# Down-weight sums called at later places, and eight tiles for the last residual loads, in an fp32 hybrid decoder layer

## The chip, the core and the metric

One core of one Trainium2 chip runs the whole program. Its engines are TensorE (PE in the trace; it loads weights as PEld), VectorE (DVE), ScalarE (ACT), GpSimd (POOL) and SyncE (SP). Each engine runs its own instructions in order and waits on semaphores for the others. The metric is the device time of one execution in microseconds, the median of the runs.

## The reference, cut to what matters

One decoder layer over 2048 tokens of width 1024, all in float32. The `mixer` part is a gated spatial unit (8 heads) beside a chunkwise matrix-memory LSTM (4 heads); then comes a channel mixer with a causal convolution over 2 x 2816 columns, then a gated embedding and a last norm.

```python
h = rms_norm(x, g_mix[i])
u, v, qk, vm, o, ig, fg = jnp.split(h @ w_in[i], cuts, axis=-1)
...
x = x + jnp.concatenate([gm, ml], axis=-1) @ w_out[i]
h = rms_norm(x, g_ffn[i])
up = causal_dwconv(h @ w_up[i], ffn_conv_w[i], ffn_conv_b[i])
a, bv = jnp.split(up, 2, axis=-1)
x = x + (jax.nn.silu(a) * bv) @ w_down[i]
gate = jax.nn.sigmoid(rms_norm(x, g_ple[i]) @ w_ple_gate[i])
x = x + gate * (p[i] @ w_ple[i])
```

## The kernel before

**Products.** Every float32 matrix is split into a high and a low part (ScalarE copies the high part, DVE subtracts it from the original to get the low one), and every product is three matmuls: high by high, high by low, low by high.

**Mixer.** A loop `b` = 0 to 3 takes 512 tokens at a time. In each block come four token groups (`w_v` columns, evacuated to `gv`, `vm1`, `osig` and the gates `gt`), the gate chain, then the query/key and `u` tiles with four heads (state update `cn`, denominators `dd`, head output `hc`), and the out-projection: eight steps `d`, each with one `w_out` slice, a load of the residual `xr` from `xT` (L681), the DVE add of residual and product (L682), and a store of the result to `x1s` (L683). Block 0 takes its input unnormed and puts the norm on while it evacuates, so it has more DVE work than the others. In the course of a block the squares and the norm of the next block's input are made (`xs` loads, `sq`, `sh`, `sl`). The eight residual tiles of a block rotate through two buffers with the tag `xr`.

**FFN.** 1024 tokens at a time: `up_half(0)`, `down_half(0)`, `up_half(1)`, `down_half(1)`. An up half runs over 22 columns `j` of 128; each `j` is computed by seven products of halves in place of eight (a Strassen form), in the order 1, 2, 6, 5, 7, 3, 4. The operands of its products are the split up weights `sw` (from `wr`, with adds at L803, L804 and L808) and the split inputs `tt` (from `hx`, which holds stored sums `td` of the normed input). After products DVE works on the results `ua` and `ub` (L855, L861 and others), makes the convolution (`fc`) and, for each pair of columns, the sums `two` of the activations, which go to memory as `ad`. For j = 8, 10, 12, 14 the step `last_in` prepares the FFN input of the last mixer block (`xl`, `hl`, further `two` tiles).

**Sums of the down weights.** The down halves use the same seven-product form and need sums of `w_down`: for each of 11 pairs `k`, `sums_load(k)` loads two 512 KB slices into two tiles `ds0`, `ds1` (one buffer each, L256) and `sums_make(k)` makes four sums of 128x512 on DVE (L262 to L265) and stores them, 256 KB each, to `sd_3`, `sd_5`, `sd_6`, `sd_7` (L267). `down_half` reads them later. They are called three in a block: 3b and 3b+1 at the token groups 1 and 3, and 3b+2 among the heads.

**What sets the order.** The Tile scheduler lists each engine's instructions. It takes an instruction as soon as its inputs and its buffers are free by its own reckoning, so a call's place in the code is not its place on an engine. Loads go through SP's queue (`DMA = nc.sync`), nearly all stores through POOL's (`ST = nc.gpsimd`); a store that waits holds what stands behind it on POOL, and so does a load on SP. A tile that is reused waits for all readers of its last contents, stores to memory included. Tiles of the FFN lie in the storage that the mixer's tiles had.

Of the kernel before, what the change touches and what calls it, by code (L numbers as in the profile page):

```python
# [9 lines left out]
F32 = mybir.dt.float32  # L10
# [5 lines left out]
P = 128  # L16
# [25 lines left out]
def trunk_kernel(ctx: ExitStack, tc: tile.TileContext, xT, pT, w_u, w_qk, w_v0, w_v1,  # L42
# [208 lines left out]

    def sums_load(k):
        if k < NJ // 2:
            dsum[k] = [big.tile([P, 2, TB], F32, tag=f"ds{i}", name=f"ds{i}") for i in range(2)]
            for i, t in enumerate(dsum[k]):
                DMA.dma_start(t, w_down[2 * k + i].rearrange("p (i t) -> p i t", t=TB))  # L256

    def sums_make(k):

        if k < NJ // 2:  # L260
            p, q = dsum.pop(k)
            V.tensor_tensor(q[:, 1, :], p[:, 1, :], q[:, 1, :], ALU.add)  # L262
            V.tensor_tensor(p[:, 1, :], p[:, 0, :], p[:, 1, :], ALU.subtract)
            V.tensor_tensor(p[:, 0, :], q[:, 1, :], p[:, 0, :], ALU.subtract)
            V.tensor_tensor(q[:, 0, :], q[:, 0, :], p[:, 0, :], ALU.subtract)  # L265
            for n, t in ((5, q[:, 1, :]), (7, p[:, 1, :]), (6, p[:, 0, :]), (3, q[:, 0, :])):
                ST.dma_start(sds[n][:, k, :], t)  # L267

    with mx:
# [3 lines left out]
        def tt(nm, dt=F32):  # L273
            return tp.tile([P, TB], dt, tag="t", name=nm, bufs=NT)
# [69 lines left out]
        for b in range(NB):  # L344
# [117 lines left out]

            sums_load(3 * b)
            ps = tok_group(1, {0: [chain1], 1: [chain2], 2: [chain3]} | ({3: [pend[0].st2]} if b else {}))
# [3 lines left out]

            sums_make(3 * b)
            ps = tok_group(2, ({2: [nx.st2]} if b + 1 < NB else {}) | ({1: [pend[0].st3]} if b else {}))  # L470
# [12 lines left out]
            for t in range(CPB):  # L483
                V.tensor_scalar(gv[:, t, :], gv[:, t, :], mu[:, t, 0:1], lrs[:, t:t + 1], ALU.subtract, ALU.mult)
            sums_load(3 * b + 1)
            ps = tok_group(3)
            for t in range(CPB):
                evac(osig[:, t, 128:512], ps[t][:, 0:384], t)
            sums_make(3 * b + 1)
            if b:  # L490
# [131 lines left out]
            k1, o0 = qk_tile(5, lambda f: head_b(*a, f))  # L622
            sums_load(3 * b + 2)
            g1 = u_tile(1)
# [4 lines left out]
            k2, o1 = qk_tile(6, lambda f: head_b(*a, f))  # L629
            sums_make(3 * b + 2)  # L630
            g2 = u_tile(2)
# [40 lines left out]
            nf = SumSq(tp, "t", NT, V)  # L672
            for d in range(KD):
                if d < 2:
                    ps = first[d][0]
                else:
                    w = wsplit(w_out[d], 1024)
                    ps = acc()
                    wide(ps, w, cat, (4, 5, 6, 0, 1, 2, 3, 7))
                xr = tp.tile([P, TB], F32, tag="xr", name="xr")  # L680
                DMA.dma_start(xr, xT[b, :, d, :])  # L681
                V.tensor_tensor(xr, xr, ps, ALU.add)  # L682
                ST.dma_start(x1s[b][:, d, :], xr)  # L683
                if b + 1 < NB:
                    nf.add(xr)
# [12 lines left out]
    with ExitStack() as fx:  # L698
# [22 lines left out]
        def pairs(t):  # L721
            return t.rearrange("p (i t) -> p i t", t=HALF)
# [366 lines left out]
        def last_in(kk):  # L1089
            xs = pairs(slot("f", "xl"))  # L1090
            DMA.dma_start(xs, x1s[NB - 1][:, kk::4, :])
            ffn_in(NB - 1, kk, xs, nl.rB, lambda: pairs(slot("f", "hl")), Twos())
# [3 lines left out]
        def at(j, prod, *fns):  # L1096
            ex.setdefault((j, prod), []).extend((0, f) for f in fns)
# [9 lines left out]
        for kk in range(4):  # L1107
            at(8 + 2 * kk, 5, lambda kk=kk: last_in(kk))
        up_half(0, ex)

# [99 lines left out]
```

## Time and profile before

| | us |
|---|---|
| median of three runs | 2453.43 (2449.56 to 2454.45) |
| the profiled execution, its own time | 2455.57 |
| span of its trace, first to last instruction | 2453.8 |
| TensorE busy | 2364.9 (96% of the span) |
| DVE busy | 1812.2 (74%) |
| ScalarE busy | 1101.4 (45%) |
| GpSimd busy | 205.8 (8%) |
| mean granted TensorE clock | 0.984 of full |

The profile is that of one execution. The chain of waits, followed back from the last instruction, lies on PE for 68% of the span, on DMA for 11%, on DVE for 11%. The timeline of an engine gives each instruction's start and length in microseconds, and in brackets how long the engine stood idle before it and what ended that. The windows give, for a stretch, the busy time of an engine and the clock that TensorE was granted. The mixer's block 0 runs from the start to about 275 us, the mixer ends at about 906 us, and up half 0 ends at about 1345 us.

### The profile page before, as it was taken

To read this page: it belongs to the slowest core of one execution; us is meant where nothing else is said; L and a number is where in the kernel's file an instruction comes from. 1 tells how busy PE (TensorE), PEld (TensorE's weight loads), DVE (VectorE), ACT (ScalarE), POOL (GpSimd) and SP (SyncE) were. 2 spreads that over 40 slices of the span, in tenths; PEclk is the share of its full clock that TensorE was granted. 3 is DMA by queue.
4 is the path that set the end of the run, shared out by engine and by line. 5 is a ranking of instruction groups with operands and counts; after the bars stand their busy time and mean duration, and the time that the engine had idled before them with its cause. 6 is when DMAs were issued, how large, how long until landed. Compare 5 with 4: busy or idle time off the path is not lost.

```text
span 2453.8 us, 31415 instructions
## 1 busy us (share of the span) xinstructions
PE 2364.9 (96%) x11336; PEld 2003.6 (82%) x11336; DVE 1812.2 (74%) x3107; ACT 1101.4 (45%) x1848; POOL 205.8 (8%) x339
## 2 busy tenths in 40 slices
PE   8989999998999999999999999999999999999998
PEld 8877898897799877878888778788888877888887
DVE  7687667766856758888987666888888865675665
ACT  3344246335524635444444555444444445553323
POOL 1111110011001000011100000010001000000000
PEclk9999999999999999999999999999999999999999
DMA  7645552645254244345434777433323367671211
GB/s 251 213 143 193 189 168 69 205 137 183 81 167 153 70 167 162 126 148 174 176 108 142 242 263 254 169 115 107 108 99 121 120 222 261 209 258 59 69 69 69
DMA packets 145245, 382.72 MB, mean 156 GB/s; under 512 B 17344, under 2 KB 19520, under 8 KB 144064
## 3 DMA queue, kind: packets, MB, share of 16 engines
q1 hardware_dynamic: 118704, 291.16, 36.5%
q0 software_dynamic: 26240, 89.15, 9.3%
q8 instruction: 89, 1.46, 0.2%
q14 instruction: 68, 0.56, 0.1%
q10 hardware_dynamic: 144, 0.40, 0.1%
HBM read 283.12 MB, written 97.52 MB: 155 GB/s over the span
## 4 chain that ended last, share of the span: by engine, by line
PE 68%; DMA 11%; DVE 11%; issue 6%; ACT 2%; POOL 1%; SPq 1%; DVEq 0%; POOLq 0%; ACTq 0%
PE ub L825 5%; PE ub L827 5%; PE ub L826 5%; PE ua L825 4%; PE ua L826 4%; PE ua L827 4%; DMA hx<-td 3%; PE gt L125 3%; PE acc L125 3%; PE gt L124 3%; PE gt L127 3%; PE acc L124 3%; PE acc L127 3%; PE acc L370 2%; PE acc L372 2%
## 5 line engine op out<-in xcount | busy, mean ns | idle before, releaser
L825 PE MATMUL ub<-tt,sw 128*128 128x512 f32 x704 | 275.8, 392 | 7.7 <-ACT tt L738 4.8
L826 PE MATMUL ub<-tt,sw 128*128 128x512 f32 x704 | 275.6, 391 | 3.1 <-DVE tt L739 3.1
L827 PE MATMUL ub<-tt,sw 128*128 128x512 f32 x704 | 275.3, 391 | 0.0
L744 ACT ACTIVATE sw<-wr 128x1024 fp32r<-128x1024 f32 x132 | 140.1, 1061 | 293.7 <-PE ua L826 246.9
L825 PE MATMUL ua<-tt,sw 128*128 128x512 f32 x528 | 206.7, 392 | 1.3 <-ACT sn L831 0.8
L826 PE MATMUL ua<-tt,sw 128*128 128x512 f32 x528 | 206.3, 391 | 0.0
L827 PE MATMUL ua<-tt,sw 128*128 128x512 f32 x528 | 206.1, 390 | 0.0
L370 PE MATMUL acc<-whi,hh 128*128 128x384 f32 (+1 forms) x512 | 176.2, 345 | 17.6 <-ACT vm L381 6.8
L117 DVE TENSOR_TENSOR wlo<-wst,whi 128x1024 fp32r<-128x1024 f32 (+2 forms) x144 | 158.7, 1105 | 43.8 <-PE acc L127 22.9
L371 PE MATMUL acc<-wlo,hh 128*128 128x384 f32 (+1 forms) x512 | 175.7, 344 | 1.0 <-DVE wlo L117 1.0
L372 PE MATMUL acc<-whi,hl 128*128 128x384 f32 (+1 forms) x512 | 174.9, 343 | 0.0
L745 DVE TENSOR_TENSOR sw<-wr,sw 128x1024 fp32r<-128x1024 f32 x132 | 161.3, 1222 | 14.5 <-ACT sw L744 12.8
L825 PEld LDWEIGHTS ub<-tt,sw 128*128 128x128 f32 x704 | 132.6, 188 | 38.8 <-ACT tt L738 5.7
L826 PEld LDWEIGHTS ub<-tt,sw 128*128 128x128 f32 x704 | 132.8, 189 | 31.4 <-DVE tt L739 3.9
L827 PEld LDWEIGHTS ub<-tt,sw 128*128 128x128 f32 x704 | 132.8, 189 | 27.4
L937 PE MATMUL da<-dt,dw 128*128 128x512 f32 x352 | 139.6, 397 | 7.0 <-DVE dt L739 7.0
L936 PE MATMUL da<-dt,dw 128*128 128x512 f32 x352 | 138.4, 395 | 4.9 <-ACT dt L738 4.9
L739 DVE TENSOR_TENSOR dt<-sx,dt 128x512 fp32r<-128x512 f32 x154 | 106.1, 689 | 49.5 <-ACT dt L738 49.4
L739 DVE TENSOR_TENSOR dw<-sx,dw 128x512 fp32r<-128x512 f32 x154 | 105.9, 688 | 44.7 <-ACT dw L738 44.5
L938 PE MATMUL da<-dt,dw 128*128 128x512 f32 x352 | 138.7, 394 | 0.0
L113 ACT ACTIVATE whi<-wst 128x1024 fp32r<-128x1024 f32 x80 | 84.3, 1058 | 104.3 <-PE acc L372 36.9
L738 ACT ACTIVATE dw<-sx 128x512 fp32r<-128x512 f32 x154 | 96.0, 623 | 78.0 <-DMA sx<-w_down 23.6
(336 smaller groups left out, 5778.5 us busy)
## 6 DMA issues: line engine op xcount, KB each, us to landing
wr<-w_up SPq DMA_DIRECT2D x44, 512.0 KB, 3.6
wr<-w_up SPq DMA_DIRECT2D x88, 256.0 KB, 5.0
act<-fc POOLq DMA_DIRECT2D x44, 512.0 KB, 5.7
ad<-two POOLq DMA_DIRECT2D x88, 256.0 KB, 4.7
sx<-sd SPq DMA_DIRECT2D x88, 256.0 KB, 3.9
sx<-ad SPq DMA_DIRECT2D x88, 256.0 KB, 4.2
wst<-w_v SPq DMA_DIRECT2D x48, 384.0 KB, 3.2
sx<-w_down SPq DMA_DIRECT2D x66, 256.0 KB, 4.2
```

The lines of the kernel that those rows point to most:

```text
L117: (leng or V).tensor_tensor(lo[:, :n], st[:, :n], hi[:, :n].bitcast(F32), ALU.subtract)
L124: PE.matmul(ps, wh, mh, start=(i == 0), stop=False)
L125: PE.matmul(ps, wh, ml, start=False, stop=False)
L127: PE.matmul(ps, wl, mh, start=False, stop=(i == n - 1))
L370: PE.matmul(ps[t][:, :n], a_h, rh, start=(k == 0), stop=False)
L371: PE.matmul(ps[t][:, :n], a_h, rl, start=False, stop=False)
L372: PE.matmul(ps[t][:, :n], a_l, rh, start=False, stop=(k == KD - 1))
L739: V.tensor_tensor(t[:, HALF:], x, t[:, :HALF].bitcast(F32), ALU.subtract)
L745: V.tensor_tensor(lo, x, hi.bitcast(F32), ALU.subtract)
L825: PE.matmul(ps, hi[:, c], t[:, :HALF], start=first, stop=False, skip_group_check=on)
L826: PE.matmul(ps, hi[:, c], t[:, HALF:], start=False, stop=False, skip_group_check=on)
L827: PE.matmul(ps, lo[:, c], t[:, :HALF], start=False, stop=last, skip_group_check=on)
```

## The change

`sums_load` takes the source of its two tiles as an argument, and both functions lose the test of `k`. The calls at the token groups and among the heads are taken out. In the out-projection of block 1 the sum 0 is made at step 3, in block 2 the sum 1 at step 3, in block 3 the sums 2 to 5 at steps 1, 3, 5 and 7; each is loaded two steps earlier into `ds0`, `ds1`. The sums 6 to 10 are called in up half 0, at j = 11, 13, 15, 17 and 19: loaded ahead of product 2, made ahead of product 3, in tiles of the tag `x`, which has four slots of 4 KB and also serves `hx`, `two` and others. In the last block the residual tiles take the tag `t` (eight buffers) in place of `xr` (two).

```diff
@@ -249,22 +249,23 @@
 
     dsum = {}
 
-    def sums_load(k):
-        if k < NJ // 2:
-            dsum[k] = [big.tile([P, 2, TB], F32, tag=f"ds{i}", name=f"ds{i}") for i in range(2)]
-            for i, t in enumerate(dsum[k]):
-                DMA.dma_start(t, w_down[2 * k + i].rearrange("p (i t) -> p i t", t=TB))
+    def sums_load(k, new):
+        dsum[k] = [new(i) for i in range(2)]
+        for i, t in enumerate(dsum[k]):
+            DMA.dma_start(t, w_down[2 * k + i].rearrange("p (i t) -> p i t", t=TB))
+
+    def ds_tile(i):
+        return big.tile([P, 2, TB], F32, tag=f"ds{i}", name=f"ds{i}")
 
     def sums_make(k):
 
-        if k < NJ // 2:
-            p, q = dsum.pop(k)
-            V.tensor_tensor(q[:, 1, :], p[:, 1, :], q[:, 1, :], ALU.add)
-            V.tensor_tensor(p[:, 1, :], p[:, 0, :], p[:, 1, :], ALU.subtract)
-            V.tensor_tensor(p[:, 0, :], q[:, 1, :], p[:, 0, :], ALU.subtract)
-            V.tensor_tensor(q[:, 0, :], q[:, 0, :], p[:, 0, :], ALU.subtract)
-            for n, t in ((5, q[:, 1, :]), (7, p[:, 1, :]), (6, p[:, 0, :]), (3, q[:, 0, :])):
-                ST.dma_start(sds[n][:, k, :], t)
+        p, q = dsum.pop(k)
+        V.tensor_tensor(q[:, 1, :], p[:, 1, :], q[:, 1, :], ALU.add)
+        V.tensor_tensor(p[:, 1, :], p[:, 0, :], p[:, 1, :], ALU.subtract)
+        V.tensor_tensor(p[:, 0, :], q[:, 1, :], p[:, 0, :], ALU.subtract)
+        V.tensor_tensor(q[:, 0, :], q[:, 0, :], p[:, 0, :], ALU.subtract)
+        for n, t in ((5, q[:, 1, :]), (7, p[:, 1, :]), (6, p[:, 0, :]), (3, q[:, 0, :])):
+            ST.dma_start(sds[n][:, k, :], t)
 
     with mx:
         tp = mx.enter_context(tc.tile_pool(name="mtmp", bufs=2))
@@ -460,13 +461,11 @@
                 stream(xT[b + 1], lambda k, x: nx.add(x))
                 nx.st1()
 
-            sums_load(3 * b)
             ps = tok_group(1, {0: [chain1], 1: [chain2], 2: [chain3]} | ({3: [pend[0].st2]} if b else {}))
             for t in range(CPB):
                 evac(gv[:, t, 0:256], ps[t][:, 128:384], t)
                 evac(vm1[:, t, 3, 0:128], ps[t][:, 0:128], t)
 
-            sums_make(3 * b)
             ps = tok_group(2, ({2: [nx.st2]} if b + 1 < NB else {}) | ({1: [pend[0].st3]} if b else {}))
             mu = sm.tile([P, CPB, 2], F32, tag="mu", name="mu")
             for t in range(CPB):
@@ -482,11 +481,9 @@
             G.tensor_tensor(lrs, lrs, mhalf, ALU.pow)
             for t in range(CPB):
                 V.tensor_scalar(gv[:, t, :], gv[:, t, :], mu[:, t, 0:1], lrs[:, t:t + 1], ALU.subtract, ALU.mult)
-            sums_load(3 * b + 1)
             ps = tok_group(3)
             for t in range(CPB):
                 evac(osig[:, t, 128:512], ps[t][:, 0:384], t)
-            sums_make(3 * b + 1)
             if b:
                 pend[1]()
             for t in range(CPB):
@@ -620,14 +617,12 @@
             a = head_a(0, q0, k0)
             mix(0, g0)
             k1, o0 = qk_tile(5, lambda f: head_b(*a, f))
-            sums_load(3 * b + 2)
             g1 = u_tile(1)
             q2 = qk_tile(2)
             a = head_a(1, q1, k1)
             mix(1, g1)
             head_out(*o0)
             k2, o1 = qk_tile(6, lambda f: head_b(*a, f))
-            sums_make(3 * b + 2)
             g2 = u_tile(2)
             q3 = qk_tile(3)
             a = head_a(2, q2, k2)
@@ -670,14 +665,21 @@
                 stream(xT[b + 1], split)
 
             nf = SumSq(tp, "t", NT, V)
-            for d in range(KD):
+            turn = {1: {3: 0}, 2: {3: 1}, 3: {1: 2, 3: 3, 5: 4, 7: 5}}.get(b, {})
+            for d in range(-2, KD):
+                if d in turn:
+                    sums_make(turn[d])
+                if d + 2 in turn:
+                    sums_load(turn[d + 2], ds_tile)
+                if d < 0:
+                    continue
                 if d < 2:
                     ps = first[d][0]
                 else:
                     w = wsplit(w_out[d], 1024)
                     ps = acc()
                     wide(ps, w, cat, (4, 5, 6, 0, 1, 2, 3, 7))
-                xr = tp.tile([P, TB], F32, tag="xr", name="xr")
+                xr = tp.tile([P, TB], F32, tag="xr", name="xr") if b + 1 < NB else tt("xr")
                 DMA.dma_start(xr, xT[b, :, d, :])
                 V.tensor_tensor(xr, xr, ps, ALU.add)
                 ST.dma_start(x1s[b][:, d, :], xr)
@@ -1106,6 +1108,9 @@
         at(7, 3, nl.st3)
         for kk in range(4):
             at(8 + 2 * kk, 5, lambda kk=kk: last_in(kk))
+        for i, k in enumerate(range(6, NK)):
+            at(11 + 2 * i, 2, lambda k=k: sums_load(k, lambda i: pairs(slot("x", "ds"))))
+            at(11 + 2 * i, 3, lambda k=k: sums_make(k))
         up_half(0, ex)
 
         ex = {}
```

The scheduler's order, not the calls' places, decides where this lands. On DVE in block 0, in the first heads, before (L262 and L263 are the first two adds of sum 6, `cn` is a head's state, `nu` and `dd` its denominator):

```order
216 L613 TENSOR_TENSOR catl<-gm,cath 128x512
217 L557 SCALAR_TENSOR_TENSOR cn_274<-cn_274,ex,pm 128x130
218 L517 COPY ub<-qhalo 128x3
219 L262 TENSOR_TENSOR ds_4540<-ds_4539,ds_4540 128x512
220 L560 SCALAR_TENSOR_TENSOR nu<-pm,ex,nu 128x130
221 L557 SCALAR_TENSOR_TENSOR cn_274<-cn_274,ex,acc 128x130
222 L562 TENSOR_SCALAR dd<-nu,ex 128x1
223 L263 TENSOR_TENSOR ds_4539<-ds_4539 128x512
224 L563 TENSOR_SCALAR dd<-nu,dd 128x1
```

The same place on DVE after:

```order
217 L610 TENSOR_TENSOR catl<-gm,cath 128x512
218 L554 SCALAR_TENSOR_TENSOR cn_274<-cn_274,ex,pm 128x130
219 L514 COPY ub<-qhalo 128x3
220 L554 SCALAR_TENSOR_TENSOR cn_274<-cn_274,ex,acc 128x130
221 L557 SCALAR_TENSOR_TENSOR nu<-pm,ex,nu 128x130
222 L557 SCALAR_TENSOR_TENSOR nu<-acc,ex,nu 128x130
223 L559 TENSOR_SCALAR dd<-nu,ex 128x1 x2
224 L560 TENSOR_SCALAR dd<-nu,dd 128x1 x2
225 L561 RECIPROCAL dd<-dd 128x1
```

Sum 6 is gone from there, and so are the sums 7 to 10 behind it. The sums 0 to 5 are still issued in block 0: the last add of sum 5 stands at row 206 of this list, in the same half of block 0.

On SP at the last out-projection, before (`xr` is the residual, `wr` the first up weights, `hx` the inputs of the first products):

```order
171 L110 DMA wst<-w_out 128x1024 x7
172 L681 DMA xr<-xT 128x512 x2
173 L110 DMA wst<-w_out 128x1024
174 L681 DMA xr<-xT 128x512 x4
175 L790 DMA wr<-w_up 128x1024
176 L791 DMA wr<-w_up 128x512
177 L792 DMA wr<-w_up 128x512
178 L779 DMA hx<-td_1_89 128x1024 x2
```

and after:

```order
155 L110 DMA wst<-w_out 128x1024 x6
156 L683 DMA xr<-xT 128x512 x8
157 L110 DMA wst<-w_out 128x1024 x2
158 L792 DMA wr<-w_up 128x1024
159 L793 DMA wr<-w_up 128x512
160 L794 DMA wr<-w_up 128x512
161 L781 DMA hx<-td_1_89 128x1024 x2
```

All eight residual loads now stand in one piece ahead of the last two `w_out` slices, and `wr` and `hx` follow without a residual load that waits for a buffer. On DVE at the end of the same out-projection, with the semaphores that each instruction waits for (DMASW are the counters of POOL's stores, DMAHW those of SP's loads), before:

```order
1369 L682 TENSOR_TENSOR xr_8312<-xr_8312,acc_8287 128x512 [waits DMASW4_49,DMAHW0_49,DVE_49,PE_49]
1370 L682 TENSOR_TENSOR xr_8347<-xr_8347,acc_8322 128x512 [waits DMASW5_49,DMAHW1_49,DVE_49,PE_49]
1371 L745 TENSOR_TENSOR sw_8439<-wr_8370,sw_8438 128x1024 [waits DMAHW2_49,Activation_49]
1372 L803 TENSOR_TENSOR wr_8370<-wr_8370 128x512 [waits DMAHW4_49,DMAHW3_49]
1373 L804 TENSOR_TENSOR wr_8370<-wr_8370 128x512 [waits DVE_49]
```

and after:

```order
1349 L684 TENSOR_TENSOR xr_8244<-xr_8244,acc_8219 128x512 [waits DMAHW4_49,PE_49]
1350 L684 TENSOR_TENSOR xr_8287<-xr_8287,acc_8262 128x512 [waits DMAHW5_49,PE_49]
1351 L747 TENSOR_TENSOR sw_8379<-wr_8310,sw_8378 128x1024 [waits DMASW3_49,DMASW6_49,DMASW0_49,DMAHW0_49,DVE_49,Activation_49]
1352 L805 TENSOR_TENSOR wr_8310<-wr_8310 128x512 [waits DMAHW2_49,DMAHW1_49]
1353 L806 TENSOR_TENSOR wr_8310<-wr_8310 128x512 [waits DVE_49]
```

The low part `sw` of the first up weight now also waits for stores. It lies at 187.9 to 191.9 KB of each partition's storage, and the residual tiles of the steps 2, 4 and 7 reach into that piece (from 189.0, 187.0 and 191.0 KB, 2 KB each); DMASW3 counts the store of step 7, the last. In the program before, the residual tiles lie elsewhere (213 to 217 KB).

On DVE in up half 0, the second of the three pairs that also have `last_in` (j = 12 and 13), before:

```order
1473 L863 TENSOR_TENSOR ua<-ua,sn 128x512
1474 L803 TENSOR_TENSOR wr<-wr 128x512
1475 L745 TENSOR_TENSOR sw<-wr,sw 128x1024
1476 L841 SCALAR_TENSOR_TENSOR fc<-ua,col,fc 128x1023
1477 L804 TENSOR_TENSOR wr<-wr 128x512
1478 L841 SCALAR_TENSOR_TENSOR fc<-ua,col,fc 128x1022
1479 L841 SCALAR_TENSOR_TENSOR fc<-ub,col,fc 128x1023
1480 L739 TENSOR_TENSOR sw<-wr,sw 128x512
1481 L841 SCALAR_TENSOR_TENSOR fc<-ub,col,fc 128x1022
1482 L855 TENSOR_TENSOR ua<-ua,sn 128x512
1483 L867 TENSOR_TENSOR fc<-fc 128x1024
1484 L745 TENSOR_TENSOR sw<-wr,sw 128x1024
```

and after (`ds` is the sum 7, its first add at L263):

```order
1454 L865 TENSOR_TENSOR ua<-ua,sn 128x512
1455 L263 TENSOR_TENSOR ds<-ds 128x512
1456 L747 TENSOR_TENSOR sw<-wr,sw 128x1024
1457 L843 SCALAR_TENSOR_TENSOR fc<-ua,col,fc 128x1023
1458 L264 TENSOR_TENSOR ds<-ds 128x512
1459 L843 SCALAR_TENSOR_TENSOR fc<-ua,col,fc 128x1022
1460 L843 SCALAR_TENSOR_TENSOR fc<-ub,col,fc 128x1023
1461 L741 TENSOR_TENSOR sw<-wr,sw 128x512
1462 L843 SCALAR_TENSOR_TENSOR fc<-ub,col,fc 128x1022
1463 L857 TENSOR_TENSOR ua<-ua,sn 128x512
1464 L869 TENSOR_TENSOR fc<-fc 128x1024
1465 L747 TENSOR_TENSOR sw<-wr,sw 128x1024
```

Two of the sum's adds stand where the weight adds of the next column stood (L803 and L804, now L805 and L806, which come later). The two tiles of this sum have the storage of the two `two` tiles of the pair before, and their loads on SP wait for those tiles' stores.

## Rows read from the trace of the kernel before

**Rows 1.** the page, part 1: engine, busy us, share of the span, instructions

```profile
PE 2364.9 (96%) x11336; PEld 2003.6 (82%) x11336; DVE 1812.2 (74%) x3107; ACT 1101.4 (45%) x1848; POOL 205.8 (8%) x339
```

**Rows 2.** timeline of TensorE, block 0: start, us, engine, line, operation [idle before <-releaser]

```profile
31.76 0.44 PE L370 MATMUL acc<-whi,hh 128*128 128x384 f32 x1 [2.71 <-ACT vm L381]
...
76.55 0.66 PE L370 MATMUL acc<-whi,hh 128*128 128x384 f32 x1 [3.35 <-DVE osig L379]
...
155.81 0.59 PE L556 MATMUL pm<-cn,qk 128*128 128x130 f32 x1 [3.74 <-DVE cn L557]
...
183.10 0.49 PE L556 MATMUL pm<-cn,qk 128*128 128x130 f32 x2 [1.70 <-DVE cn L557]
...
196.17 0.48 PE L583 MATMUL acc<-ident,hc 128*128 128x128 f32 x1 [1.50 <-DVE hc L576]
...
275.39 0.69 PE L370 MATMUL acc<-whi,hh 128*128 128x384 f32 x1 [4.06 <-ACT vm L381]
```

**Rows 3.** timeline of DVE in the same stretch, the same columns

```profile
69.83 0.69 DVE L262 TENSOR_TENSOR ds<-ds,ds 128x512 f32<-128x512 f32 x1 [5.23 <-DMA ds<-w_down]
...
154.54 0.69 DVE L262 TENSOR_TENSOR ds<-ds,ds 128x512 f32<-128x512 f32 x1 [4.55 <-DMA ds<-w_down]
...
181.83 0.69 DVE L262 TENSOR_TENSOR ds<-ds,ds 128x512 f32<-128x512 f32 x1 [2.27 <-DMA ds<-w_down]
...
262.93 0.69 DVE L262 TENSOR_TENSOR ds<-ds,ds 128x512 f32<-128x512 f32 x1 [5.78 <-DMA ds<-w_down]
```

**Rows 4.** windows: start:end, length, TensorE busy (instructions), granted clock, DMA share, GB/s

```profile
76.00:80.00 4.00, 3.45 (x11) 0.57 0.52 182
152.00:164.00 12.00, 8.26 (x27) 0.72 0.23 88
184.00:188.00 4.00, 4.00 (x20) 1.00 0.35 131
196.00:204.00 8.00, 7.83 (x35) 0.57 0.68 251
272.00:284.00 12.00, 8.61 (x37) 0.72 0.53 184
480.00:520.00 40.00, 40.00 (x235) 1.00 0.41 132
```

**Rows 5.** timeline of DVE, POOL and TensorE at the entry to the FFN

```profile
906.54 1.22 DVE L745 TENSOR_TENSOR sw<-wr,sw 128x1024 fp32r<-128x1024 f32 x1
...
906.92 0.54 POOL L683 DMA_DIRECT2D x1s<-xr  x1 [4.90 <-DVE xr L682]
...
907.62 0.50 PE L825 MATMUL ub<-tt,sw 128*128 128x512 f32 x1 [1.72 <-ACT tt L738]
...
911.01 0.80 PE L826 MATMUL ub<-tt,sw 128*128 128x512 f32 x1 [2.89 <-DVE tt L739]
...
924.78 0.51 PE L825 MATMUL ub<-tt,sw 128*128 128x512 f32 x1 [3.11 <-ACT tt L738]
```

**Rows 6.** line L683, its last four stores: microseconds from issue to landing

```profile
DMA to landing us min/median/max: 2.3/3.7/7.4
```

**Rows 7.** timeline of POOL, DVE and TensorE in one pair of up half 0

```profile
1165.41 0.54 POOL L882 DMA_DIRECT2D ad<-two  x1 [0.67 <-DVE two L880]
...
1171.72 0.68 DVE L803 TENSOR_TENSOR wr<-wr 128x512 f32<-128x512 f32 x1
...
1179.41 0.69 DVE L855 TENSOR_TENSOR ua<-ua,sn 128x512 f32<-128x512 f32 x1
...
1181.79 0.39 PE L825 MATMUL ua<-tt,sw 128*128 128x512 f32 x1
...
1187.50 0.70 DVE L861 TENSOR_TENSOR ub<-ub,sn 128x512 f32<-128x512 f32 x1 [0.70 <-PE ub L827]
```

**Rows 8.** the page, part 6: issue, count, KB each, median us to landing

```profile
ad<-two POOLq DMA_DIRECT2D x88, 256.0 KB, 4.7
```

**Rows 9.** line L256, its 22 loads: microseconds from issue to landing

```profile
DMA to landing us min/median/max: 3.5/4.6/7.6
```


## What I predicted, before the change was run

> **What bounds the kernel now.** I read the busy shares first: TensorE works 2364.9 us of a span of 2453.8 us [rows 1], so about 89 us are all that any reordering can win, and only where TensorE itself stands still. Next I read TensorE's timeline for its idle times. Several of the longest lie in the first 290 us, in block 0 and at its border to block 1; the six that this change can touch are in [rows 2]: 2.71, 3.35, 3.74, 1.70, 1.50 and 4.06 us. Then I read DVE's timeline just ahead of each. Four of them follow a DVE add of the down-weight sums that waited for its own load: 5.23, 4.55, 2.27 and 5.78 us [rows 3]. DVE runs in order, so everything queued behind such an add (the evacuation `osig`, the state update `cn`, the squares of the next block's norm) stands with it, and TensorE behind that. Last I read the granted clock, in windows [rows 4]. After the 3.74 us idle it fell, and 12 us at a mean of 0.72 cost 12 x 0.28 = 3.4 us; after the 4.06 us idle the same 3.4; over 196 to 204 us, at 0.57, again 8 x 0.43 = 3.4; after the 3.35 us idle 4 x 0.43 = 1.7. After the idle of 1.70 us it stayed at 1.00. The full level is 2.4 GHz, the lower 1.2. So a stall costs its own length and, if it is long enough, some 3 us more.
>
> The times below are changes against the profiled execution (2455.57 us around its span); I apply them to the median of the runs, 2453.43 us, 2.14 below it.
>
> **What the change really moves.** All eleven sums of before run in block 0, wherever the code calls them, since the scheduler may start them as soon as their two tiles are free. The same holds after: the six sums that are now called in the out-projections of blocks 1 to 3 are issued in block 0 again, about where the first six stood. Only the last five leave, for up half 0. Instruction counts are unchanged. Blocks 1 to 3 keep their order but for the last out-projection's residual loads.
>
> **Gains in block 0, step by step.**
> - The stop at 155.81: the sum whose add waited 4.55 us is gone from there, and nothing else stood between DVE and `cn`. 3.74 + 3.4 of clock = 7.1 at most; a next-late input could keep 2. I take 7 (5 to 7.1).
> - The stops at 183.10 and 196.17: 1.70 behind the add that waited 2.27, and 1.50 with 3.4 of clock behind a head's output `hc`, where two more adds stood on DVE. 6.6 at most; `hc` also ends a chain of its own, so I take 4 (2 to 7).
> - The block border at 275.39: the sum behind the 5.78 us wait goes, its three later adds too (3 x 0.69 [rows 3]), and two loads leave SP ahead of the next block's input. 4.06 + 3.4 = 7.5. That the border can run without a stop is shown by the next two, where TensorE is busy for all 40 us of 480 to 520 [rows 4]. I take 7 (4 to 7.5).
> - The stop at 76.55: the add behind it moves later, but the sum before it, itself later now, waits for its own load in turn, since that load waits for the stores of the first: I put that stall at 2 us, an estimate between none and the 5.23 of [rows 3]. 3.35 + 1.7 = 5.1 at most; I take 3 (0 to 5.1).
> - The stop at 31.76: the first sum's adds and store leave its front. Ends 0 and 2.71; the rows leave it open, I take the middle, 1.5.
>
> Sum of gains: 7 + 4 + 7 + 3 + 1.5 = 22.5 (11 to 29).
>
> **Costs.**
> - Entry to the FFN. The eight residual tiles now lie in the storage of which the first up weight's low part (`sw`) takes a piece, so this DVE instruction gains a wait for the store of the last residual. In before it ran at 906.54, straight behind the last add; that store is issued at 906.92 [rows 5] and the last four landed 2.3 to 7.4 us after issue, the short ones with no loads beside them [rows 6]. After the change the four first `hx` loads are long through, because the eight residual loads no longer hold SP up, so I take 2.3: `sw` starts at 909.2, 2.7 us late. Behind it on DVE stand the weight adds and the `tt` that TensorE waits for at 911.01 already; nothing absorbs it. The earlier loads don't help, since the fifth `hx` needs a tile that the first `tt` free, which stand in the same queue. 2.7 (1 to 5.4).
> - Up half 0. In the three pairs that also prepare the last block's input (j = 11, 13, 15), the sum's two tiles are those of the pair before's activation sums. Read for the pair around 1175 us [rows 7]: the last of their stores is issued at 1165.41 and lands 4.7 us later by the median [rows 8], 1170.1; the second of the two loads is issued right behind, say at 1170.5, and takes 4.6 [rows 9]: 1175.1. DVE is at the place of the first add at 1171.72 and stalls 3.4 us. The two adds that come before `ua` stand where two weight adds of 0.68 stood, which now come later. So `ua`, 1179.41 before, comes 3.4 later; it has 0.69 to run and TensorE wants it at 1181.79, a slack of 1.7: TensorE stops 1.7 us. The two adds left, 1.4 us, meet an idle of 0.70 ahead of `ub` (1187.50): up to 0.5 more. 2.2 x 3 = 6.6. A stop of this length left the clock at 1.00 at 183.10. In the two later pairs (j = 17, 19) the tiles have long been free, and four adds, 2.8 us, meet that idle and the slack ahead of `ua`, 0.70 + 1.7: 0 to 0.5 each. Together 7 (1 to 11).
> - The moved stores go through POOL, which has nothing else urgent there, and the moved loads stand ahead of the next up weights on SP, whose tiles come free later than 1170 in any case. Nothing.
>
> Net: 22.5 - 2.7 - 7 = 12.8 faster: 2453.4 - 12.8 = **2440.6 us**; its own range, with the terms not all at one end, 2434 to 2448.
>
> **A rule against a row.** The term that hangs on landings goes by rows: 4.7 for a 256 KB store and 4.6 for a 512 KB load, which the POOL and SP queues give in this very stretch. The Trainium skill ("DMA: Bandwidth & Descriptors", section "Anatomy of one DMA — SWDGE (gpsimd) path") states a fixed 2.0 us, mostly the confirmation of the last byte, plus bytes over 436 GB/s, an estimate of 2.6 for the store and 4.4 for two loads together; with these, the loads would land at 1172.8, DVE would stall 1 us, inside the slack, and the time would be near 2435. The median of this case is longer for the store and agrees for the load, so I go by the rows.
>
> **Rivals.**
> - Quick landings. If the store lands in 2.3 us [rows 6] and the load in 3.5 [rows 9], the second load is there at 1171.6 and no pair stops: the up half costs 1 instead of 7. 2453.4 - 22.5 + 2.7 + 1 = 2434.6. For it: queues move as stalls shift. Against it: both medians. Chance 0.14.
> - The up half takes it all (slower). DVE is nearly full there. If the second load takes the longest landing seen, 7.6 [rows 9], the stall is 6.4, TensorE stops 4.7 + 0.5, and the clock falls as after 3.74 us, 3.4 more: 8.6 a pair, 26 for three, 27 with the others. 2453.4 - 22.5 + 2.7 + 27 = 2460.6. It decides from about 8 us a pair; a stop over some 3 us is where it begins. For it: loads, stores and weight loads share that stretch. Against it: 7.6 is the worst of 22. Chance 0.13.
> - Block 0 gives little back. The adds go, but the heads' own chain, the next block's input or the remaining six sums end the same stops a little later; the gains are at their low bounds, 11 to 12. 2453.4 - 12 + 2.7 + 7 = 2451. For it: six of eleven sums stay, in the denser half. Against it: blocks 2 and 3 run the same code without these stops. Chance 0.19.
> - The residual tiles do shorten the entry. If `sw` were not held by that store, the earlier loads would take the 1.72 and 3.11 us stops at 907.62 and 924.78 [rows 5] and perhaps 1.7 of clock: 6.5 gained instead of 2.7 lost, 2440.6 - 9.2 = 2431. Against it: the tiles overlap. Chance 0.08.
>
> **How the numbers follow.** Forecast 0.46, the others as given. About 0.2%, 4.9 us, is what a measurement of this kernel can tell from no change. Faster: forecast, quick landings and short entry, 0.68, less the forecast's slow tail and plus the quick edge of the block-0 rival: 0.70. Slower 0.12, the rest, 0.18, within. The range 2429 to 2456 leaves out most of the slow rival and the sum of all good ends.
>
> **What would show it.** Right: no idle over 1 us on TensorE at 150 to 160 and 265 to 280, and a clock of 1.00 at both; `sw` at the entry 2 to 3 us behind the last residual add, and TensorE's next stop there longer by as much; three stops of 1.5 to 2.5 us on TensorE between 1130 and 1260, behind `ua`, with DVE waiting for `ds` some 8 us before. Wrong: the border stop still there with another releaser, stops over 3 us in up half 0 with the clock down, or adds of the sums in blocks 1 to 3.

## The result, and the profile after

The changed kernel takes 2436.69 us (median of 4 runs, 2436.01 to 2442.41) beside 2453.94 us for the kernel before in the same session: a ratio of 0.9938, 95% interval 0.9919 to 0.9958, so 15 us (10 to 20) less by the ratio and 17.25 by the medians. The forecast was 12.8 less. The profiled executions, on which everything below rests, are 2455.57 and 2436.01 us, with spans of 2453.8 and 2434.3: 19.5 apart.

To see where the time went I cut both traces at marks that DVE leaves in the same order in each: the last residual add of the mixer, and the first add on `ub` (L861 before, L863 after) in columns 0, 8, 16 and 21 of up half 0. The lengths of the stretches, in us:

| stretch | before | after | gain |
|---|---|---|---|
| start to last residual add (mixer) | 905.9 | 869.4 | 36.5 |
| to the first `ub` (entry to the FFN) | 26.8 | 32.1 | -5.3 |
| columns 0 to 8 of up half 0 | 158.9 | 158.0 | 0.9 |
| columns 8 to 16 | 153.3 | 166.3 | -13.0 |
| columns 16 to 21 | 95.1 | 94.8 | 0.3 |
| the rest, to the end of the span | 1113.7 | 1113.7 | 0.0 |

So the mixer gave back nearly twice the net, and two places took half of that away again. In block 0 the stops of [rows 2] are gone or short. TensorE's timeline after (start, us, engine, line, operation, idle before and its releaser) has these as the longest that are left there behind the program's start:

```profile
70.22 0.41 PE L371 MATMUL acc<-whi,hh 128*128 128x384 f32 x1 [1.18 <-DVE osig L380]
...
122.38 0.38 PE L553 MATMUL acc<-cn,qk 128*128 128x130 f32 x1 [1.42 <-DVE cn L554]
...
193.17 0.33 PE L580 MATMUL acc<-ident,hc 128*128 128x128 f32 x1 [1.98 <-DVE hc L573]
```

The windows of the kernel after, over the places where [rows 4] had 0.72 (start:end, length, TensorE busy, granted clock, DMA share, GB/s), are full or nearly so, at the full clock. The instruction of the 155.81 us stop now stands at 145.0, that of 183.10 at 166.7, and that of the block border, 275.39, at 245.5, where the third window meets the fourth:

```profile
140.00:160.00 20.00, 20.00 (x116) 1.00 0.21 76
160.00:180.00 20.00, 19.26 (x117) 1.00 0.20 57
225.00:245.00 20.00, 20.00 (x111) 1.00 0.73 239
245.00:265.00 20.00, 20.00 (x122) 1.00 0.32 97
```

At the entry, the answer to [rows 5] (DVE, POOL and TensorE around 870 us, the same columns): `sw` no longer starts 0.6 us after the last residual add, but 4.15, of which 3.46 is its wait for the store, and TensorE stops for 7.31 where it had stopped for 1.72 and 2.89.

```profile
869.40 0.69 DVE L684 TENSOR_TENSOR xr<-xr,acc 128x512 f32<-128x512 f32 x1 [4.75 <-PE acc L127]
873.55 1.23 DVE L747 TENSOR_TENSOR sw<-wr,sw 128x1024 fp32r<-128x1024 f32 x1 [3.46 <-DMA x1s<-xr]
...
870.98 0.54 POOL L685 DMA_DIRECT2D x1s<-xr  x1 [5.50 <-DVE xr L684]
...
878.02 0.79 PE L828 MATMUL ub<-tt,sw 128*128 128x512 f32 x1 [7.31 <-DVE tt L741]
```

In up half 0, the answer to [rows 7]: DVE's wait for a sum's load in the first of the three dense pairs, and TensorE's stop behind it. The next two pairs show waits of 3.69 and 5.56 us and the two stops below.

```profile
1105.35 0.69 DVE L263 TENSOR_TENSOR ds<-ds 128x512 f32<-128x512 f32 x1 [3.50 <-DMA ds<-w_down]
...
1113.81 0.79 PE L827 MATMUL ua<-tt,sw 128*128 128x512 f32 x1 [2.46 <-DVE ua L857]
...
1156.06 0.50 PE L827 MATMUL ua<-tt,sw 128*128 128x512 f32 x1 [2.42 <-DVE ua L857]
...
1198.98 0.79 PE L827 MATMUL ua<-tt,sw 128*128 128x512 f32 x1 [4.24 <-DVE ua L857]
```

### The profile page after: what moved, and what is told of

It reads as the page before. It is cut to its first block, busy times and chain, and to the rows that moved or that the text cites. A ratio compares the mean times of both kernels' runs of the same rounds, so it can differ in the third digit from the quotient of the medians.

```text
span 2434.3 us, 31406 instructions
## 1 busy us (share of the span) xinstructions
PE 2351.1 (97%) x11336; PEld 1991.0 (82%) x11336; DVE 1812.8 (74%) x3107; ACT 1101.9 (45%) x1848; POOL 205.7 (8%) x339
## 4 chain that ended last, share of the span: by engine, by line
PE 64%; DMA 11%; issue 11%; DVE 11%; ACT 2%; POOL 1%; SPq 1%; DVEq 0%; POOLq 0%; ACTq 0%
PE ub L827 4%; PE ub L828 4%; PE ub L829 4%; DMA hx<-td 4%; PE acc L124 3%; PE acc L125 3%; PE acc L127 3%; PE ua L827 3%; PE ua L828 3%; PE gt L124 3%; PE gt L127 3%; PE gt L125 3%; PE ua L829 3%; PE acc L371 3%; PE acc L372 3%
## 5 line engine op out<-in xcount | busy, mean ns | idle before, releaser
L740 ACT ACTIVATE dt<-sx 128x512 fp32r<-128x512 f32 x154 | 96.2, 625 | 72.0 <-PE db L940 34.4
```

The lines of the kernel that those rows point to most:

```text
L740: A.activation(t[:, :HALF], x, AF.Copy)
```

## The experiments

The stretch times of the kernels, by the same marks (profiled execution, us), and the comparison with the kernel before on the same chip (ratio of medians, 95% interval). Identical code differs from execution to execution. The kernels "after", "sums later" (twice) and "columns 16 to 20" have the same code up to the entry's end, and took 869.4 to 871.4 for the mixer and 29.7 to 32.1 for the entry. The rest is the same code in all of them and took 1111.2 to 1115.8.

| kernel | mixer | entry | 0-8 | 8-16 | 16-21 | rest | median | ratio |
|---|---|---|---|---|---|---|---|---|
| before | 905.9 | 26.8 | 158.9 | 153.3 | 95.1 | 1113.7 | 2453.9 | 1 |
| after | 869.4 | 32.1 | 158.0 | 166.3 | 94.8 | 1113.7 | 2436.7 | 0.9938 (0.9919 to 0.9958) |
| after, residuals back | 870.6 | 26.6 | 159.6 | 166.9 | 94.5 | 1112.8 | 2434.2 | 0.9911 (0.9896 to 0.9926) |
| after, sums later | 871.4 | 29.9 | 159.1 | 152.6 | 94.9 | 1111.2 | 2421.5 | 0.9860 (0.9846 to 0.9875) |
| after, columns 16 to 20 | 870.6 | 29.7 | 157.8 | 153.2 | 109.3 | 1115.5 | 2436.9 | 0.9920 (0.9905 to 0.9934) |
| before, eight tiles alone | 904.5 | 26.3 | 158.6 | 153.6 | 95.1 | 1112.9 | 2452.6 | 0.9988 (0.9970 to 1.0006) |
| later, residuals back | 872.1 | 26.3 | 157.8 | 153.0 | 94.8 | 1115.8 | 2421.4 | 0.9880 (0.9864 to 0.9897) |
| later, last residual apart | 873.2 | 26.5 | 158.1 | 153.8 | 94.6 | 1114.2 | 2420.3 | 0.9878 (0.9863 to 0.9893) |
| sums later, again | 871.0 | 29.7 | 158.0 | 153.7 | 94.6 | 1113.8 | 2425.1 | 0.9883 (0.9865 to 0.9902) |
| later, residuals back, again | 872.2 | 26.6 | 158.6 | 153.0 | 94.6 | 1113.0 | 2420.0 | 0.9866 (0.9846 to 0.9887) |
| later, seven sums in mixer | 878.1 | 25.2 | 159.5 | 154.4 | 94.7 | 1113.6 | 2428.2 | 0.9902 (0.9878 to 0.9925) |
| later, five sums in mixer | 872.5 | 28.7 | 157.6 | 154.0 | 94.8 | 1114.1 | 2425.4 | 0.9883 (0.9865 to 0.9902) |

**The entry: is it the tiles?** Undo that part of the change:

```diff
-                xr = tp.tile([P, TB], F32, tag="xr", name="xr") if b + 1 < NB else tt("xr")
+                xr = tp.tile([P, TB], F32, tag="xr", name="xr")
```

> The changed kernel with one part undone: the last block's residual tiles rotate through the two buffers of the tag xr again; the sums stay at their new places. Theory A: the 3.46 us that the first weight's low part (sw) waits at the entry to the FFN for the last residual's store, and the extra 1.7 us of lower clock behind it, are the tiles' doing, 5.3 us in all; so the time falls from 2436.7 to about 2431.5, and sw runs straight behind the last residual add. Rival: the entry costs what it costs for another reason (the inputs hx, the second half's work), and the early loads help elsewhere: no change, 2436.7, or slower.

The entry fell to 26.6 us, that of before, and `sw` runs straight behind the last add, so the wait belongs to the tiles. Its price is nearer 3 us than 5.3: the three other executions with the same code up to there took 29.7 to 29.9. The time was 2434.2, less of a gain than forecast. The same part alone, put into the kernel before (the diff the other way round):

> The kernel before with that one part alone: the last block's residuals in eight tiles of the tag t, all eleven sums where they were. Theory A: sw waits for the last store here too, 3 to 3.5 us, TensorE's stop behind it grows as much and the clock is low for longer: 2453.9 + 5 = 2459. Rival: the tiles cost only with the other order of the changed kernel, or the early loads shorten the entry: 2454 or below.

This missed. Entry 26.3, time 2452.6, no cost. `sw` has no wait there; DVE's timeline of that run:

```profile
904.52 0.69 DVE L682 TENSOR_TENSOR xr<-xr,acc 128x512 f32<-128x512 f32 x1 [4.75 <-PE acc L127]
905.12 1.22 DVE L745 TENSOR_TENSOR sw<-wr,sw 128x1024 fp32r<-128x1024 f32 x1
```

In that kernel the last residual lies at 181 to 183 KB of the storage and `sw` at 187.9 to 191.9: the pieces under `sw` are those of steps 1, 2 and 4, stored long before. The eight buffers are given out in turn, as a ring. Which of them the last residual gets is the turn of that ring, and in the changed kernel it fell on the wrong one. Two kernels further below bear this out without having been made for it: with seven or with five sums in the mixer the ring stands elsewhere, the last residual lies at 181 or 183 KB, and `sw` does not wait, though all eight tiles have the tag `t`. With seven:

```profile
878.08 0.69 DVE L684 TENSOR_TENSOR xr<-xr,acc 128x512 f32<-128x512 f32 x1 [4.75 <-PE acc L127]
878.69 1.22 DVE L747 TENSOR_TENSOR sw<-wr,sw 128x1024 fp32r<-128x1024 f32 x1
```

So what costs is one overlap, not the eight tiles. That can be tested by taking only the last residual out of the ring (on top of the later sums, below):

```diff
-                xr = tp.tile(...) if b + 1 < NB else tt("xr")
+                xr = tp.tile(...) if b + 1 < NB or d == KD - 1 else tt("xr")
```

> The sums made two products later, the first seven residuals of the last block in the eight tiles of the tag t, and only the last residual in a tile of the tag xr. Theory A': what costs at the entry is one overlap, the last residual's tile with the storage of sw; the early loads cost nothing and bring nothing. Then sw runs straight behind the last add, the entry takes 26.3 to 26.8 us as in the kernel before, and the time equals that of the kernel with all residuals back, 2417 to 2419. Rival (early loads of residuals and inputs do shorten the entry once sw is free): entry below 25, time 2415 or less. Rival (any tile of the tag t costs): entry about 30, time 2421.

Entry 26.5, time 2420.3, above the range but about 1 us below all residuals back on the same chip (2421.4). Seven early loads gain nothing that can be seen over the rotation, and without the overlap of that one tile the wait is gone.

**Up half 0: the wait or the work?** The sums are made two products later, and nothing else changes:

```diff
-            at(11 + 2 * i, 3, lambda k=k: sums_make(k))
+            at(12 + 2 * i, 1, lambda k=k: sums_make(k))
```

> The changed kernel with the five sums of up half 0 made two products later (ahead of product 1 of the next column in place of product 3), loads and pairs unchanged. Theory B: TensorE's three stops of 2.4, 2.4 and 4.2 us come from DVE waiting 3.5 to 5.6 us for the sum's load; two products are 5.4 us, so the load is there, the stops go and 10 to 12 us with them: about 2425 to 2427. Rival: DVE is full in these pairs and the four adds themselves, 2.4 us, are too much wherever they stand: 3 us or less comes back, 2434 or above.

Columns 8 to 16 went from 166.3 to 152.6, even under the 153.3 of before, with the four adds of each sum still in these pairs. The time fell to 2421.5, further than forecast; the same kernel took 2425.1 in a later session, so the surplus is not the edit's. The first add in that run, DVE's timeline, with no wait ahead of it:

```profile
1113.05 0.69 DVE L880 TENSOR_TENSOR two<-fc 128x512 f32<-128x512 f32 x1
1113.65 0.69 DVE L263 TENSOR_TENSOR ds<-ds 128x512 f32<-128x512 f32 x1
```

So DVE was not full. The edit moves the adds in DVE's order and takes away their wait, both at once. That the place alone costs little is seen in the changed kernel itself: at column 17, a pair without `last_in`, the first add stands ahead of product 3 as in the other pairs, waits 0.09 us, and columns 16 to 21 take 94.8 us (95.1 before). The other way to the same end, columns with less work:

```diff
-            at(11 + 2 * i, 2, lambda k=k: sums_load(k, ...))
-            at(11 + 2 * i, 3, lambda k=k: sums_make(k))
+            at(16 + i, 2, lambda k=k: sums_load(k, ...))
+            at(16 + i, 3, lambda k=k: sums_make(k))
```

> The changed kernel with the five sums at columns 16 to 20, one in each column, behind the last input step of the mixer's last block (column 14). Theory B and its rival both expect the stops at columns 11 to 15 to go. Theory B: each load has its slot early enough or costs at most 1 us: 2425 to 2427. Rival (adds too many for DVE): here there is room as well, so the same time, and only the run with the sums made later tells the two apart. A third possibility: with a sum in every column the four slots turn faster, loads wait for stores again and stops of 1 to 3 us come in columns 17 and 19: 2430.

The third possibility came, and larger: columns 8 to 16 are free (153.2), columns 16 to 21 take 109.3 in place of 94.8. The loads are closer together and wait for slots; DVE and TensorE in column 17 of that run:

```profile
1221.62 0.69 DVE L263 TENSOR_TENSOR ds<-ds 128x512 f32<-128x512 f32 x1 [5.76 <-DMA ds<-w_down]
...
1229.48 0.79 PE L827 MATMUL ua<-tt,sw 128*128 128x512 f32 x1 [4.99 <-DVE ua L857]
```

In columns 16, 18 and 20 of the same run the adds wait at most 0.60 us, and TensorE has no stop over 0.5 us there. A pair with little other work does not help when the add is next in order and its data is not there.

**Are the two costs independent?** Both edits at once:

> The changed kernel with both edits that helped alone: the residuals rotate through two tiles of the tag xr as before, and the five sums of up half 0 are made two products later. If the two costs are independent, as theories A and B say, the entry to the FFN takes 26.6 us from the last residual add to the first ub as in the run with the tiles undone (32.1 changed), columns 8 to 16 take 152.6 us (166.3 changed), and the time is 2421.5 less 2.5 to 5: 2416.5 to 2419. If they interact (the earlier entry moves the stalls), 2421 or above.

The stretches say yes (entry 26.3, columns 8 to 16 at 153.0), the median of 2421.4 does not: it is that of the kernel with only the sums later, but from another chip. Between the two traces the rest, which is the same code, differs by 4.6 us (1111.2 and 1115.8), more than the entry's gain. Both once more, side by side on one chip:

> The changed kernel with the five sums of up half 0 made two products later, the same kernel as before, now beside the one with the residuals put back on the same chip. The stretch times of the two gave 3.4 to 3.6 us less for the entry with the residuals back, the medians of two different chips nothing. Theory A (the wait at the entry is paid in full): this one is 3 to 4 us above the other. Rival (the entry's gain is given back in the stretches behind it): the two agree within 1 us.

> The sums made two products later and the residuals back in two tiles of the tag xr, beside the run without the second edit. Theory A: 3 to 4 us below it. Rival: the same within 1 us.

There the medians were 2425.1 (four runs, 2422.5 to 2429.0) and 2420.0 (five runs, 2417.1 to 2428.7), the entries 29.7 and 26.6, the rests 1113.8 and 1113.0, so there the gain is not given back. The direction and the size fit, but the two ratios, 0.9883 (0.9865 to 0.9902) and 0.9866 (0.9846 to 0.9887), overlap. That the stretch itself is 3 to 5 us shorter is shown in every pair of traces; that all of it reaches the total is likely, not shown.

**Block 0: what did a sum cost there?** The adds of the sums 6 to 10 left out of the kernel before, their loads and stores kept:

```diff
+            if k < 6:
                 V.tensor_tensor(q[:, 1, :], p[:, 1, :], q[:, 1, :], ALU.add)
...
```

> The kernel before with the DVE adds of the sums 6 to 10 left out; their loads and stores stay on SP and POOL in block 0 (the stored values are then the plain halves, so the output is not the reference's). Theory C: what made block 0 long is DVE standing in order behind a load; without the adds nothing on DVE waits for those loads, so the stops at 155.8, 183 and 275 go, with their clock, and the mixer to its last residual add takes about 872 to 878 us (905.9 before, 869.4 changed). Rival: the loads themselves, 5 MB on SP ahead of weights and inputs, hold the block: the mixer stays at 895 or more, the stop at 275 above all.

The mixer took 893.5 us (one run, 2443.5 us in all), outside both expectations and 1.5 us short of the rival's bound. The border to block 1 lost its stop (no stop of TensorE over 0.7 us from 217 to 429 us), as my theory has it and against the rival's main sign. But inside block 0 there are new stops. POOL's, DVE's and TensorE's timeline of that run:

```profile
167.29 1.07 POOL L268 DMA_DIRECT2D sd<-ds  x2 [1.42 <-DMA ds<-w_down]
168.38 1.03 POOL L574 TENSOR_TENSOR sr<-sr,mhalf 128x4 f32<-128x4 f32 x1
...
169.44 0.29 DVE L577 TENSOR_SCALAR hc<-hc,sr 128x128 f32<-128x128 f32 x1 [6.33 <-POOL sr L574]
...
171.70 0.38 PE L540 MATMUL pm<-qk 128*128 128x128 f32 x1 [3.88 <-ACT qk L532]
```

Without adds, the stores on POOL wait for the loads themselves, and a head's norm `sr`, four columns of work on the same engine, stands behind them; DVE then waits 6.33 us for `sr`. The wait only changed its queue. The run with the adds of the sums 0 to 5 left out of the changed kernel (the same edit, `if k >= 6`) shows it more strongly:

> The changed kernel with the DVE adds of the sums 0 to 5 left out, loads and stores kept (output not the reference's). It asks what the six sums that stayed in block 0 still cost. Theory C: TensorE's stops that are left in block 0 are of 0.6 to 2 us and mostly of the heads' own chain, so 2 to 4 us at most come off the mixer: 865 to 868 against 869.4. Rival: they still hold the block up in places the idle times don't show: 860 or less.

With less work the mixer took 881.6, 12 us more (one run, 2444.9 us in all). The norm `nr` on POOL stood behind the stores, DVE waited 8.40 us for it, and TensorE stopped for 7.48 us. So neither run could answer its question. They show that it matters in which queue the wait stands; what the adds' own work costs they do not show.

The question was then put by moving one sum at a time. One back into the mixer:

```diff
-            turn = {1: {3: 0}, 2: {3: 1}, 3: {1: 2, 3: 3, 5: 4, 7: 5}}.get(b, {})
+            turn = {1: {3: 0}, 2: {3: 1, 7: 2}, 3: {1: 3, 3: 4, 5: 5, 7: 6}}.get(b, {})
...
-        for i, k in enumerate(range(6, NK)):
+        for i, k in enumerate(range(7, NK), 1):
```

> The sums of up half 0 made two products later, and the sum 6 back in the mixer (seven there, four in up half 0). Theory C: each sum costs what TensorE's stop behind its load's wait costs; the seventh again stands on DVE ahead of a state update at about 150 us, where it cost 3.74 us and 3.4 us of clock: the mixer takes 876 to 879 us in place of 870 to 872, the time 2427 to 2429. Rival (block 0 only gets long when the later sums all come, by traffic or by the sum of DVE work): 1 to 2 us.

The mixer took 878.1, 7.1 more than the 871.0 of its neighbour on that chip. The sum stands where it stood before, with the wait and the stop:

```profile
148.65 0.69 DVE L263 TENSOR_TENSOR ds<-ds,ds 128x512 f32<-128x512 f32 x1 [3.92 <-DMA ds<-w_down]
...
149.92 0.38 PE L553 MATMUL pm<-cn,qk 128*128 128x130 f32 x1 [3.10 <-DVE cn L554]
```

The stop and 1.7 us of lowered clock behind it are 4.8 us. The two kernels are 5.5 us apart at the first residual add of block 0 and 5.0 at that of block 1. The rest comes in block 2, where no sum is made: a stop of 7.21 us in place of 6.48, and 5.1 us of lowered clock around it in place of 3.4. So the mixer's time lies in the forecast range partly by chance. In the medians only 3.1 us show (2428.2 and 2425.1), with overlapping ranges, since in this kernel `sw` has no wait and the entry is 4.5 us shorter.

One more out of the mixer (`range(5, NK)`, from column 9 on, and no sum 5 at step 7):

> The sums of up half 0 made two products later, and one more sum moved there (five in the mixer, six in up half 0 from column 9 on). Theory C: the sum 5 waits for its load without a long stop of TensorE behind it (1.42 us is the largest there), so at most 1.5 us come off the mixer, and the sum costs next to nothing in up half 0: 2419.5 to 2421.5. Rival (every sum in block 0 costs alike): 5 to 7 us come off, 2415.

The mixer took 872.5 beside 871.0: nothing gained. The time was 2425.4 beside 2425.1, so the two agree; the range of 2419.5 to 2421.5 had been counted from the earlier session's 2421.5. The seventh sum costs about 5 us, the sixth nothing that can be seen. These two moves fit a sum that costs what TensorE's stop behind its wait costs; the other sums were not moved singly. The waits of the sums 3 to 5 (3.39, 2.48 and 1.86 us in the changed kernel) have no stop over 1.42 us behind them.

**A version that beats both.** The sums later, with the residuals back or only the last one apart, takes 2420 to 2421 us, 0.9866 to 0.9880 of the kernel before. The sums later alone had 0.9860 and 0.9883, so the ratios do not set the two apart.

## Why the prediction was right, and where it was not

**Sign and mechanism were right.** The five sums left block 0 and its stops went with them; `sw` got the wait for the last residual's store; three stops behind `ua` came in up half 0, after waits for `ds`; and the later two sums there cost nothing. But the terms were mis-sized, and the errors cancelled: by the traces, gains 14 too low, costs 9 too low. That the total came so near the forecast is in part luck. The 89 us of idle time that the prediction calls all that reordering can win left out the clock: TensorE's busy time itself fell, from 2364.9 to 2351.1 us.

**The gains, 22.5 against 36.5.** Against the marks, the offset of the changed kernel grows to 7.4 us by the first heads (122 us of before, where 1.5 + 3 had been put on the two stops), to 25.2 by the first residual add of block 0 (7 + 4), to 33.7 by that of block 1 (7 for the border), and to 36.5 by the end of the mixer (nothing). Each step gave more than I put down, for two reasons. I kept a part of every stop for a next-late input, and little came of that: after the change the longest stop in block 0 behind the start is 1.98 us. And I left clock out: 32 to 36 and 216 to 220 us of before also stood at 0.57, 1.7 us each, behind the stop at 31.76 and one of 2.45 at 215.19 that is not among the six of [rows 2]. Together the lowered stretches of block 0 and its border cost 15.4 us, and all of them are gone. In blocks 1 and 2 two lowered stretches of 1.7 us went as well, with the stops before them nearly unchanged; that was not in any step, and the two executions of the kernel with later sums have at least one of them again, so it is not the change's. Of the 36.5, 17.6 are TensorE's busy time in the mixer (858.3 and 840.7 us), the clock's share, and the remaining 19 its idle time. The three other executions with this mixer gained 34.6 to 35.3.

**The entry, 2.7 against 5.3.** The step was right, and so was the landing: the last store took the 2.3 us that I had taken for a queue without loads.

```profile
DMA to landing us min/median/max: 2.3/2.3/2.3
```

But the store was issued 1.58 us after the add's start, not 0.98, so `sw` came 3.5 later instead of 2.7. The long stop itself did not lower the clock for longer: the windows behind it sum to 3.4 us, as those of before do, and part of that falls into the stop itself (TensorE has no work from 872 to 876), where nothing is lost by it.

```profile
872.00:876.00 4.00, 0.00 (x0) 0.83 0.17 66
876.00:880.00 4.00, 1.98 (x5) 0.50 0.07 17
880.00:884.00 4.00, 4.00 (x16) 0.82 0.87 275
```

The rest of the 5.3 came with the next stop, of 4.76 us where [rows 5] had 3.11, and with the clock behind it, 3.4 us where before had 1.7:

```profile
892.89 0.80 PE L827 MATMUL ub<-tt,sw 128*128 128x512 f32 x1 [4.76 <-ACT tt L740]
...
892.00:896.00 4.00, 3.11 (x7) 0.50 0.78 309
896.00:900.00 4.00, 4.00 (x14) 0.69 0.61 185
```

The load of the `hx` for that `tt` took 7.24 us to land. In the three other executions with the same code up to there the same load took 5.8 to 5.9, `sw` waited the same 3.46 or 3.47 us, the next stop was 2.37 to 3.43, and the entry took 29.7 to 29.9, some 3 us more than before. So the 2.7 was nearly right for the wait, and about 2 of the 5.3 belong to this one execution.

**Up half 0, 7 against 13.** The chain store, load, add was right. Three terms were too small. The loads landed in 4.8 to 7.7 us after issue, median 5.5, not 4.6, so that DVE waited 3.50, 3.69 and 5.56 where 3.4 was expected. TensorE's stop was 2.4 to 4.2 where the slack of 1.7 should have left 1.7; wait less stop gives a slack of 1.0 to 1.3. And I had set the clock at nothing by the 1.70 us stop of [rows 2], while it fell behind two of these stops, of 2.46 and 4.24 us, and not behind the third, of 2.42. So the "some 3 us" at which the slow rival lets it fall is no border either:

```profile
1112.00:1116.00 4.00, 2.19 (x5) 0.69 0.75 227
1116.00:1120.00 4.00, 4.00 (x17) 0.88 0.90 304
1196.00:1200.00 4.00, 1.01 (x2) 0.86 0.51 152
1200.00:1204.00 4.00, 4.00 (x14) 0.71 0.85 326
```

The stops, 9.1 us, and two times 1.7 of clock are 12.5 of the 13.0. This is half of the slow rival (26), with its mechanism in two of the three pairs. The Trainium skill ("DMA: Bandwidth & Descriptors", section "Anatomy of one DMA — SWDGE (gpsimd) path") states its figures for DMAs of the gpsimd path, so for the stores; the estimate from them was 2.6 us, and the last store at the entry took 2.3. The estimate of 4.4 for the two loads, which go through SP, applied these figures beyond that path, and the 4.8 to 7.7 of each load in the loaded stretch do not bear it out. That the time lies near the 2435 which those figures gave is chance.

**The other rivals.** Quick landings: the median, 2436.7, is nearer to its 2434.6 than to the forecast, but its condition did not hold, since the loads landed late and three pairs stopped. Block 0 gives little back: it gave more than the forecast's sum, so that one was wrong. The early residual loads don't visibly shorten the entry even when `sw` is free: 25.2, 26.3, 26.5 and 28.7 us in the four kernels with early loads, 26.3 to 26.8 in the four with the rotation.

## What to carry to other kernels

In this kernel an operation whose data comes by DMA cost next to nothing for its own work on an engine with room; it cost what stood behind it in order while the data was not there. So look at which engine's queue carries the wait, give the load a head start of its whole landing time under load, and price the clock with every stop. The scheduler here put such work where buffers came free, not where the code calls it, so read its order. And when one stage's storage is handed to the next, the last tile written in the first can hold the first instruction of the second; which tile that is may be the turn of a ring.

## What the hardware showed that I had not expected

The length of a stop does not settle whether the clock falls behind it. In the second head output of block 2 three executions have the same stop on the same instruction, with the same program around it. TensorE before, after, and in the second run with the later sums, and the windows behind (for each, the two that hold the stop and what follows):

```profile
662.12 0.33 PE L583 MATMUL acc<-ident,hc 128*128 128x128 f32 x1 [2.63 <-DVE hc L576]
...
660.00:664.00 4.00, 1.88 (x10) 0.95 0.34 119
664.00:668.00 4.00, 4.00 (x13) 0.62 0.00 0
```

```profile
627.21 0.33 PE L580 MATMUL acc<-ident,hc 128*128 128x128 f32 x1 [2.63 <-DVE hc L573]
...
624.00:628.00 4.00, 1.37 (x9) 1.00 0.42 131
628.00:632.00 4.00, 4.00 (x19) 1.00 0.01 4
```

```profile
627.34 0.48 PE L580 MATMUL acc<-ident,hc 128*128 128x128 f32 x1 [2.63 <-DVE hc L573]
...
624.00:628.00 4.00, 1.37 (x6) 0.92 0.45 131
628.00:632.00 4.00, 4.00 (x15) 0.66 0.02 4
```

It fell from the full level, 2.4 GHz, to the half level, 1.2 GHz, for part of these windows in the first and the third and stayed at full in the second, a difference of 1.7 us for the same program stretch. What decides it was not tried.
